# A decoder block on one core: the gates of its recurrence as pairs of 64-row matmuls, their evictions by halves

## The chip, the core and the metric

The kernel runs on one core of a Trainium2 chip. TensorE (PE) multiplies matrices into PSUM; VectorE (DVE), ScalarE (ACT) and GpSimd (POOL) do the elementwise work; SyncE (SP) issues most of the DMAs, ACT and POOL a few. The engines run side by side, each through its own instructions in a fixed order, and wait for one another by semaphores. The metric is the device time of one execution in microseconds (us).

## The reference, cut to what matters

The kernel computes one decoder block on x of 2048 positions by 1024 channels, in float32: one input projection to 9216 columns, a branch of dilated attention, a branch with a gated linear recurrence, a merge, an output projection and a layer norm. The change touches the recurrence:

```python
def rg_lru(x, w_r, b_r, w_i, b_i, lam):      # w_r, w_i: (16 blocks, 64, 64)
    xb = x.reshape(B, S, 16, 64)
    r = sigmoid(einsum('bsgi,gij->bsgj', xb, w_r).reshape(B, S, C) + b_r)
    i = sigmoid(einsum('bsgi,gij->bsgj', xb, w_i).reshape(B, S, C) + b_i)
    log_a = -8.0 * r * softplus(-lam)
    a = exp(log_a)
    mult = sqrt(maximum(-expm1(2.0 * log_a), 0.0))
    u = mult * (i * x)
    # h_t = a_t * h_(t-1) + u_t over the positions
```

Both gate matrices are block-diagonal: 16 blocks of 64 channels that don't mix.

## The kernel before, in words

**Stages.** The first stage (to about 1454 us) computes the input projection in products of seven matrices for four (Strassen's scheme), and the recurrence beside it. Then come the attention, the projections of both branches, and the output with the layer norm. Each float32 operand is split into a rounded part and a rest, so every product takes three matmuls: high by high, high by rest, rest by high.

**Layout.** Channels lie on the 128 partitions, positions on the free axis, in 4 chunks of 512. The 1024 channels of the recurrence are 8 tiles of 128 (`i`), each with two of the 64-channel blocks. For each tile and chunk the coroutine `lru(i, c, ub)` does the convolution, the two gates, and the scan: 32 chains in all.

**The order.** The first stage is written out step by step. A step (a "tick") records one product of 12 matmuls (`product`, L602 is its matmul), then the loads and weight preparations that fall due (`events`), then what waiting chains may record (`run_chains`), then the eviction of the product's PSUM bank (`evacuate`). A chain yields an `Ask`: how many ticks it waits (`lag`, 1 if not given), how many free slots of SBUF it needs, and how many microseconds of ACT, DVE or POOL it means to use. `run_chains` grants it only while the budget of that tick (`left`, refilled by 2.75 us a tick for each engine) is above zero. So a changed `Ask` moves not only its own chain: what it leaves or takes of the budget moves the steps of other chains, with their DMAs. The order on each engine is then fixed.

**The gates.** A chain loads its gate weights (L438, L439) into a slot `gr` as two matrices of 128x128, each with two blocks of 64x64 on its diagonal and zeros beside them, and splits them into `gw` (L456 on ACT, L219 on DVE, the helper `tt`). It splits its input `v` into `vh` and `vl`. The matmuls are put off by one tick and recorded in the middle of a product: three for r into one PSUM bank `g`, three for i into another (L472 to L474). There are two such banks, and a flag keeps a second chain out until the first has recorded its evictions. ACT evicts both banks by tanh (L485, L486; sigmoid is made from tanh), and in the same step of the chain makes the exponential, an affine step and a second tanh of r (L487 to L489), while DVE forms (1 + ti) * v (L490). Square root (L494), scan and the rest follow in later steps.

**Other names.** `q` are the PSUM banks of the products (four of them), `hA`, `hS`, `l` the split weights of a product, `wA`, `wS` their raw loads (L226 is the helper's line for both the plain and the half-summed ones), `wl_scr` a scratch copy of `l` for the second half. `vtp` are transposes in the same stage. `s` (L981) and `o` (L1034) are matmuls of the attention, `yb` (L1281 to L1283) the projection that follows it.

Of the kernel before, what the change touches and what calls it, by code (L numbers as in the profile page):

```python
# [8 lines left out]
F32 = mybir.dt.float32  # L9
F32R = mybir.dt.float32r  # L10
AF = mybir.ActivationFunctionType
ALU = mybir.AluOpType
# [3 lines left out]
P = 128  # L16
# [4 lines left out]
CH = 512  # L21
# [10 lines left out]
def hybrid_block_kernel(ctx: ExitStack, tc: tile.TileContext, a: dict, out: bass.AP):  # L32
    nc = tc.nc
    sp, act, dve, pool, pe = nc.sync, nc.scalar, nc.vector, nc.gpsimd, nc.tensor

    def flat(t):
        return t.bitcast(F32)
# [39 lines left out]
    lr = cst.tile([P, 8, 8], F32, name="lr")  # L77
    act.dma_start(lr, a["lru_vec"])
    brh = cst.tile([P, 2, 8], F32, name="brh")
    sp2 = cst.tile([P, 8], F32, name="sp2")  # L80


# [41 lines left out]
    ps = stA.enter_context(tc.tile_pool(name="ps", bufs=2, space=PSUM))  # L124
# [93 lines left out]
    def tt(eng, out, in0, in1, op):  # L218
        eng.tensor_tensor(out=out, in0=in0, in1=in1, op=op)  # L219
# [201 lines left out]
    GLG, GW = {}, {}  # L421
# [5 lines left out]
    def lru(i, c, ub):  # L427
        nm = f"{i}_{c}"
        f = FT_U + i
# [5 lines left out]
        if bring_gw:  # L435
            yield Ask(lag=0, need=1, keep=1)
            gr = take("gr" + nm, F32)
            sp.dma_start(gr[:, 0:P], a["wr"][i])  # L438
            sp.dma_start(gr[:, P:2 * P], a["wi"][i])  # L439
        if c == 1 and i in put_off:  # L440
            yield Ask(lag=4)
        yield Ask(lag=0, need=1, keep=6, cond=lambda: gate["live"] < 2 and begun[i] == c, ACT=1.3, DVE=2.7)
# [5 lines left out]
        for j in range(1, 4):  # L448
            dve.scalar_tensor_tensor(out=v, in0=ub[:, j:j + CH], scalar=lrn[:, j, i:i + 1], in1=v,
                                     op0=ALU.mult, op1=ALU.add)  # L450
        act.activation(ubs[:, i, c + 1, 0:3], ub[:, CH:CH + 3], AF.Copy)
        ub_free.append(ub)
        if bring_gw:
            yield Ask(ACT=.4, DVE=.4, lag=2, need=1, keep=1)
            w = GW[i] = take("gw" + nm)
            act.activation(w[:, 0:2 * P], gr[:, 0:2 * P], AF.Copy)  # L456
            tt(dve, w[:, 2 * P:], gr[:, 0:2 * P], flat(w[:, 0:2 * P]), ALU.subtract)
            give(gr)
        yield Ask(lag=0, cond=lambda: gated[i] == c)
        gw = GW[i].rearrange("p (l j f) -> p l j f", l=2, j=2)  # L460
        yield Ask(need=2, keep=1, ACT=.66, DVE=.75)
        vh, vl = take("vh" + nm), take("vl" + nm)
        act.activation(vh, v, AF.Copy)
# [3 lines left out]
        pg = []  # L467

        def gates():
            for j in range(2):  # L470
                g = ps.tile([P, CH], F32, tag="g", name=f"g{j}{nm}", bufs=2)
                pe.matmul(g, gw[:, 0, j], vh, start=True, stop=False)  # L472
                pe.matmul(g, gw[:, 0, j], vl, start=False, stop=False)
                pe.matmul(g, gw[:, 1, j], vh, start=False, stop=True)  # L474
                pg.append(g)
            give(vh, vl)
            if c in ((0, 3) if i in put_off else (1, 3)):
                give(GW[i])

        pe_later(1, gates)  # L480
        gated[i] = c + 1
        yield Ask(lag=2, need=3, keep=1, ACT=3.3, DVE=.75)
        gate["busy"] = False
        tr, ti, e = take("tr" + nm, F32), take("ti" + nm, F32), take("e" + nm, F32)
        act.activation(tr, pg[0], AF.Tanh, scale=0.5, bias=brh[:, 0, i:i + 1])  # L485
        act.activation(ti, pg[1], AF.Tanh, scale=0.5, bias=brh[:, 1, i:i + 1])  # L486
        act.activation(e, tr, AF.Exp, scale=sp2n[:, i:i + 1], bias=sp2n[:, i:i + 1])  # L487
        act.activation(e, e, AF.Identity, scale=0.5, bias=half_t)
        act.activation(tr, tr, AF.Tanh, scale=sp2[:, i:i + 1], bias=sp2[:, i:i + 1])  # L489
# [3 lines left out]
        s, w = take("sq" + nm, F32), take("nw" + nm, F32)  # L493
# [12 lines left out]
        h = take("h" + nm, F32)  # L506
# [11 lines left out]
        g = GLG.pop((i, c))  # L518
# [165 lines left out]
    for s, pl in enumerate(plan):  # L684
        if pl[0] and pl[4] == "ug":
            i = pl[1][1][0] - FT_U
# [70 lines left out]
    at(base[len(seq)] - 10, drop_cs)  # L757
    at(base[len(seq)] + 12, lambda: load_cs(1))

    HALF = (slice(0, 64), slice(64, P))  # L760
    USLOT = (("X3", "X2"), ("X0", "X4"), ("Y0", "X1"))
    VSLOT = {(0, 0): "X5", (2, 0): "Y1", (1, 0): "Y2", (0, 1): "X5", (2, 1): "Y1", (1, 1): "Y2"}

# [87 lines left out]
    def consts():  # L851
        dve.tensor_scalar(out=bh, in0=b72, scalar1=0.5, scalar2=None, op0=ALU.mult)
        dve.tensor_scalar(out=bn, in0=b72, scalar1=-1.0, scalar2=None, op0=ALU.mult)
        dve.tensor_scalar(out=bq, in0=b72[:, 0:64], scalar1=0.25, scalar2=None, op0=ALU.mult)
        dve.tensor_scalar(out=brh, in0=lr[:, 5:7, :], scalar1=0.5, scalar2=None, op0=ALU.mult)
        dve.tensor_scalar(out=lrn, in0=lr[:, 0:4, :], scalar1=-1.0, scalar2=None, op0=ALU.mult)
        dve.memset(ubs, 0.0)
        dve.memset(hst, 0.0)
# [62 lines left out]
    n = len(where)  # L921
# [35 lines left out]
    def scores(i):  # L957
# [40 lines left out]
    def turn(i, w):  # L998
# [303 lines left out]
    for n in range(32):  # L1302
        c, f = divmod(n, 8)
# [223 lines left out]
```

## Time and profile before

| | |
|---|---|
| median of 3 runs | 2132.93 us (2130.52 to 2132.96) |
| profiled execution | 2130.19 us, its span 2128.4 us |
| PE busy | 2093.8 us (98% of the span), 12016 matmuls |
| DVE, ACT, POOL busy | 1672.6 (79%), 1078.8 (51%), 457.6 us (22%) |
| gate matmuls (L472 to L474) | 192, started between 111.6 and 1404.3 us |
| tanh evictions of the gates (L485, L486) | 64, 688 and 684 ns each (median) |
| loads of the activation table | 66, 1283 ns each |

In the rows of the profile a line gives start, duration, engine, source line, operation, out<-in, shapes and a count of merged instructions; in brackets stands how long the engine had been idle and what ended it. "PEld" is the weight load of a matmul, "SPq" and "ACTq" an issue of a DMA by that engine. A matmul's record goes on after the next one has started, so the pace of a stream is read from the starts.

### The profile page before, as it was taken

The numbers are of one execution on the slowest core, as the hardware profiler recorded it, in microseconds if no ns is written. First come the engines' busy times: TensorE is split into PE (matmuls) and PEld (weight loads), VectorE is DVE, ScalarE is ACT, GpSimd is POOL, SyncE is SP. The second block draws the span as 40 slices with busy tenths as digits, with TensorE's granted clock in tenths as the row PEclk, the third lists the DMA queues.
The fourth block names the chain that finished last, engine by engine and source line by source line (L and its number), as shares of the span: only waits on it lengthen the run. The fifth ranks groups of instructions, "written<-read, shape, count | busy, mean of one in ns | idle before, by whom it ended". The sixth has DMA issues, their size and how long they took to land.

```text
span 2128.4 us, 35700 instructions
## 1 busy us (share of the span) xinstructions
PE 2093.8 (98%) x12016; PEld 1745.9 (82%) x12016; DVE 1672.6 (79%) x3193; ACT 1078.8 (51%) x2284; POOL 457.6 (22%) x397
## 2 busy tenths in 40 slices
PE   8999999999999999999999999999999999999998
PEld 7888888888878888888888888888888888878887
DVE  8888889799789867787787887886999645476667
ACT  6355445357356566546557656657999411121100
POOL 1001011011011002121221221223535444332120
PEclk9999999999999999999999999999999999999999
DMA  9987997988988876677778788879998688874431
GB/s 273 275 267 218 290 261 238 272 265 250 278 271 257 305 220 196 221 226 219 249 251 270 262 256 254 256 227 383 289 310 262 210 280 281 290 246 162 163 109 70
DMA packets 348263, 525.72 MB, mean 247 GB/s; under 512 B 123568, under 2 KB 156336, under 8 KB 344240
## 3 DMA queue, kind: packets, MB, share of 16 engines
q1 hardware_dynamic: 330368, 491.64, 71.3%
q0 software_dynamic: 10080, 18.35, 5.4%
q10 hardware_dynamic: 7632, 13.44, 1.7%
q8 instruction: 96, 1.57, 0.3%
q14 instruction: 87, 0.71, 0.1%
HBM read 318.18 MB, written 190.45 MB: 239 GB/s over the span
## 4 chain that ended last, share of the span: by engine, by line
PE 60%; ACT 6%; DMA 3%; DVE 2%; issue 1%; SPq 1%; POOL 0%; DVEq 0%; ACTq 0%
PE q L602 37%; ACT p L996 4%; PE z L1393 3%; PE z L1391 3%; PE z L1392 3%; PE yb L1281 2%; PE yb L1282 2%; PE yb L1283 2%; PE o L1034 1%; ACT ptb L1019 1%; PE ya L1361 1%; PE ya L1360 1%; PE ya L1359 1%; PE s L981 1%; DMA yb_scr<-gB 1%; DVE p L988 1%
## 5 line engine op out<-in xcount | busy, mean ns | idle before, releaser
L602 PE MATMUL q<-xT,hS 128*128 128x512 f32 x1680 | 518.8, 390 | 0.0
L602 PE MATMUL q<-xT,l 128*128 128x512 f32 x1120 | 436.0, 389 | 0.0
L602 PE MATMUL q<-xB,hA 128*128 128x512 f32 x1248 | 387.3, 392 | 5.7 <-ACT xB L207 5.7
L602 PEld LDWEIGHTS q<-xT,hS 128*128 128x128 f32 x1680 | 314.1, 188 | 64.3
L602 PE MATMUL q<-xB,l 128*128 128x512 f32 x904 | 352.9, 390 | 0.5 <-DMA l<-wl_scr 0.4
L602 PEld LDWEIGHTS q<-xB,hA 128*128 128x128 f32 x1248 | 234.1, 188 | 54.4 <-ACT xB L207 5.7
L602 PEld LDWEIGHTS q<-xT,l 128*128 128x128 f32 x1120 | 210.2, 188 | 44.3
L602 PEld LDWEIGHTS q<-xB,l 128*128 128x128 f32 x904 | 170.1, 188 | 37.5 <-DMA l<-wl_scr 0.8
L264 ACT ACTIVATE hA<-wA 128x512 fp32r<-128x512 f32 x218 | 135.5, 623 | 82.1 <-DMA wA<-in_w_in_dram 44.0
L602 PE MATMUL q<-xB,hS 128*128 128x512 f32 x560 | 173.5, 391 | 2.2 <-DVE v L219 2.2
L996 ACT ACTIVATE p<-p,sta 128x256 f32<-128x256 f32 (+1 forms) x384 | 172.2, 455 | 5.9 <-DVE sta L988 5.2
L602 PE MATMUL q<-xT,hA 128*128 128x512 f32 x560 | 172.8, 390 | 0.0
L237 POOL DMA_DIRECT2D wS<-in_w_in_dram x70 | 61.1, 935 | 477.6 <-DMA wS<-in_w_in_dram 120.0
L264 ACT ACTIVATE hS<-S 128x512 fp32r<-128x512 f32 x175 | 109.0, 623 | 87.9 <-DVE S L219 48.4
L219 POOL TENSOR_TENSOR S<-S,wA 128x512 f32<-128x512 f32 x35 | 45.6, 1303 | 445.8 <-DVE S L219 319.1
L602 PEld LDWEIGHTS q<-xB,hS 128*128 128x128 f32 x560 | 104.2, 188 | 23.8 <-issue 2.6
L602 PEld LDWEIGHTS q<-xT,hA 128*128 128x128 f32 x560 | 104.7, 188 | 21.9 <-issue 0.4
L988 DVE CUSTOM_DVE_ANT_0 p<-s,mask 128x256 f32<-128x256 f32 (+1 forms) x384 | 118.8, 360 | 4.6 <-PE s L981 3.6
L1393 PE MATMUL z<-wo,ml 128*128 128x512 f32 (+1 forms) x264 | 101.1, 383 | 0.8 <-DVE ml L1378 0.8
L1391 PE MATMUL z<-wo,mh 128*128 128x512 f32 (+1 forms) x264 | 101.1, 383 | 0.1
L1392 PE MATMUL z<-wo,mh 128*128 128x512 f32 (+1 forms) x264 | 101.0, 383 | 0.0
L1281 PE MATMUL yb<-h,wl 128*128 128x512 f32 x256 | 100.3, 392 | 0.0
(199 smaller groups left out, 4182.1 us busy)
## 6 DMA issues: line engine op xcount, KB each, us to landing
wA<-in_w_in_dram SPq DMA_DIRECT2D x253, 256.0 KB, 5.0
wl_scr<-l SPq DMA_DIRECT2D x105, 512.0 KB, 5.3
l<-wl_scr SPq DMA_DIRECT2D x105, 512.0 KB, 4.8
sw<-y SPq DMA_DIRECT2D x384, 64.0 KB, 3.1
wS<-in_w_in_dram SPq DMA_DIRECT2D x70, 256.0 KB, 4.8
wS<-in_w_in_dram POOLq DMA_DIRECT2D x70, 256.0 KB, 6.4
qh_scr<-hi SPq DMA_DIRECT2D x48, 256.0 KB, 5.8
v_scr<-vs SPq DMA_DIRECT2D x48, 256.0 KB, 4.4
```

The lines of the kernel that those rows point to most:

```text
L219: eng.tensor_tensor(out=out, in0=in0, in1=in1, op=op)
L237: pool.dma_start(t, w_part(s, x), accum_op=ALU.add)
L264: act.activation(h, r, AF.Copy)
L602: pe.matmul(bank, w[:, ks], x[:, kk, xx], start=(first and i == 0), stop=(last and i == 11))
L988: dve.tensor_tensor_reduce(out=st["p", i, j][:, h, lo:256], in0=st["s", i, j // 2][h][:, j % 2, lo:256], in1=mask[:, lo:256], scale=1.0, s ...
L996: act.activation(p, p, AF.Exp, scale=-1.0, bias=s[:, h:h + 1], accum_out=s[:, 2 + h:3 + h])
L1281: pe.matmul(yb, WL[f][:, 0, k], xx[:, 0], start=(k == 0), stop=False)
L1282: pe.matmul(yb, WL[f][:, 0, k], xx[:, 1], start=False, stop=False)
L1283: pe.matmul(yb, WL[f][:, 1, k], xx[:, 0], start=False, stop=(k == 7))
L1391: pe.matmul(z, mh[:, k], w[:, 0, hs], start=(k == 0), stop=False)
L1392: pe.matmul(z, mh[:, k], w[:, 1, hs], start=False, stop=False)
L1393: pe.matmul(z, ml[:, k], w[:, 0, hs], start=False, stop=(k == 7))
```

## The change

The gate matrices are no longer padded to 128x128. The upper 64 partitions hold, side by side, the blocks of r and of i for the tile's first 64 channels; the lower 64 hold those of its second 64 channels, i first and then r. A matmul takes 64 partitions of weights and of input and fills all 128 partitions of a bank: bank 0 gets r above and i below, for the first 64 channels; bank 1 gets i above and r below, for the second 64. Six matmuls of 64 rows, alternating between the upper and the lower half, take the place of six of 128 rows.

The evictions go by halves, so that r and i each end on their own channels' partitions: four tanhs of 64x512 instead of two of 128x512, two of which read PSUM on one half of the partitions and write SBUF on the other. The biases `brh` are arranged to match by four small DMAs on ACT's queue at the start. The step of the chain that held the tanhs and what follows is cut in two: the four tanhs ask for 2.5 us of ACT, and a tick later at the earliest the exponential, the affine step, the second tanh and DVE's product ask for 2.0 us of ACT and 0.75 of DVE. The gate weights are loaded by four DMAs of 64x64 instead of two of 128x128, and their split covers half the columns.

```diff
+    HALF = (slice(0, 64), slice(64, P))
+    for hs, os in (HALF, HALF[::-1]):
+        act.dma_start(brh[hs, 0], a["lru_vec"][hs, 5])
+        act.dma_start(brh[hs, 1], a["lru_vec"][os, 6])
...
-            sp.dma_start(gr[:, 0:P], a["wr"][i])
-            sp.dma_start(gr[:, P:2 * P], a["wi"][i])
+            for hs, n in ((HALF[0], ("wr", "wi")), (HALF[1], ("wi", "wr"))):
+                for j in range(2):
+                    sp.dma_start(gr[hs, HALF[j]], a[n[j]][i, hs, hs])
...
-            yield Ask(ACT=.4, DVE=.4, lag=2, need=1, keep=1)
+            yield Ask(ACT=.25, DVE=.25, lag=2, need=1, keep=1)
             w = GW[i] = take("gw" + nm)
-            act.activation(w[:, 0:2 * P], gr[:, 0:2 * P], AF.Copy)
-            tt(dve, w[:, 2 * P:], gr[:, 0:2 * P], flat(w[:, 0:2 * P]), ALU.subtract)
+            act.activation(w[:, 0:P], gr[:, 0:P], AF.Copy)
+            tt(dve, w[:, P:2 * P], gr[:, 0:P], flat(w[:, 0:P]), ALU.subtract)
...
-            for j in range(2):
-                g = ps.tile([P, CH], F32, tag="g", name=f"g{j}{nm}", bufs=2)
-                pe.matmul(g, gw[:, 0, j], vh, start=True, stop=False)
-                pe.matmul(g, gw[:, 0, j], vl, start=False, stop=False)
-                pe.matmul(g, gw[:, 1, j], vh, start=False, stop=True)
-                pg.append(g)
+            pg[:] = [ps.tile([P, CH], F32, tag="g", name=f"g{j}{nm}", bufs=2) for j in range(2)]
+            for k, (l, x) in enumerate(((0, vh), (0, vl), (1, vh))):
+                for hs, g in zip(HALF, pg):
+                    pe.matmul(g, gw[hs, l], x[hs], start=(k == 0), stop=(k == 2))
...
-        yield Ask(lag=2, need=3, keep=1, ACT=3.3, DVE=.75)
+        yield Ask(lag=2, need=2, keep=1, ACT=2.5)
         gate["busy"] = False
-        tr, ti, e = take("tr" + nm, F32), take("ti" + nm, F32), take("e" + nm, F32)
-        act.activation(tr, pg[0], AF.Tanh, scale=0.5, bias=brh[:, 0, i:i + 1])
-        act.activation(ti, pg[1], AF.Tanh, scale=0.5, bias=brh[:, 1, i:i + 1])
+        tr, ti = take("tr" + nm, F32), take("ti" + nm, F32)
+        for h, (hs, os) in enumerate((HALF, HALF[::-1])):
+            act.activation(tr[hs], pg[h][hs], AF.Tanh, scale=0.5, bias=brh[hs, 0, i:i + 1])
+            act.activation(ti[hs], pg[h][os], AF.Tanh, scale=0.5, bias=brh[os, 1, i:i + 1])
+        yield Ask(need=1, keep=1, ACT=2.0, DVE=.75)
+        e = take("e" + nm, F32)
         act.activation(e, tr, AF.Exp, scale=sp2n[:, i:i + 1], bias=sp2n[:, i:i + 1])
...
-        dve.tensor_scalar(out=brh, in0=lr[:, 5:7, :], scalar1=0.5, scalar2=None, op0=ALU.mult)
+        dve.tensor_scalar(out=brh, in0=brh, scalar1=0.5, scalar2=None, op0=ALU.mult)
```

Source lines after the change are higher by 4 to 6 (L602 becomes L608, L219 becomes L223).

PE, the first group of gates, before. The last two numbers in a name are a chain's chunk or a product's number and the tile's number; banks 1294 and 1298 are r and i.

```order
L473 MATMUL g_0_1294<-vl_0_1224,gw_0_1200 128x512
L474 MATMUL g_0_1294<-vh_0_1223,gw_0_1200 128x512
L472 MATMUL g_0_1298<-vh_0_1223,gw_0_1200 128x512
L473 MATMUL g_0_1298<-vl_0_1224,gw_0_1200 128x512
L474 MATMUL g_0_1298<-vh_0_1223,gw_0_1200 128x512
L602 MATMUL q_5_1287<-xT_423,hS_5_1192 128x512 x2
```

The same group on PE now:

```order
L478 MATMUL g_0_1301<-vh_0_1229,gw_0_1206 128x512
L478 MATMUL g_0_1300<-vl_0_1230,gw_0_1206 128x512
L478 MATMUL g_0_1301<-vl_0_1230,gw_0_1206 128x512
L478 MATMUL g_0_1300<-vh_0_1229,gw_0_1206 128x512
L478 MATMUL g_0_1301<-vh_0_1229,gw_0_1206 128x512
L608 MATMUL q_5_1293<-xT_427,hS_5_1198 128x512 x2
```

The first gate matmul stands ahead of each piece. The group has kept its place in the product; its matmuls now alternate between the banks.

ACT, the evictions of that group and what follows them, before (`hA`, `hS` are weight copies for coming products, which PE waits for in the end):

```order
L485 ACTIVATE tr_0_1342<-g_0_1294,brh 128x512
L486 ACTIVATE ti_0_1343<-g_0_1298,brh 128x512
L487 ACTIVATE e_0_1344<-tr_0_1342,sp2n 128x512
L488 ACTIVATE e_0_1344<-e_0_1344,half_t 128x512
L489 ACTIVATE tr_0_1342<-tr_0_1342,sp_201 128x512
L264 ACTIVATE hA_6_1372<-wA_6_1251 128x512
L494 ACT_TABLE_LOAD
```

The same place on ACT now:

```order
L489 ACTIVATE tr_0_1348<-g_0_1300,brh 64x512
L490 ACTIVATE ti_0_1349<-g_0_1300,brh 64x512
L489 ACTIVATE tr_0_1348<-g_0_1301,brh 64x512
L490 ACTIVATE ti_0_1349<-g_0_1301,brh 64x512
L268 ACTIVATE hA_6_1375<-wA_6_1257 128x512
L493 ACTIVATE e_0_1380<-tr_0_1348,sp2n 128x512
L494 ACTIVATE e_0_1380<-e_0_1380,half_t 128x512
L495 ACTIVATE tr_0_1348<-tr_0_1348,sp_205 128x512
```

Four tanhs stand where two stood, and the weight copy that came after the second tanh of r now comes before the exponential. The number of table loads is 66 as before.

SP at the last gate load of the first half, before (`k_scr` and `ql_scr` are stores of keys and queries, `gr7` the gate weights of tile 7, `wA22_32` and `wA12_32` weights of product 32):

```order
L339 DMA ql_scr6_100<-rp6_0_6303 128x512
L325 DMA k_scr6_101<-rp18_1_6329 128x512
L438 DMA gr7_0_6360<-in_wr_dram 128x128
L439 DMA gr7_0_6360<-in_wi_dram 128x128
L226 DMA wA22_32_6382<-in_w_in_dram 128x512
L226 DMA wA12_32_6384<-in_w_in_dram 128x512
```

The same place on SP now:

```order
L343 DMA ql_scr6_100<-rp6_0_6341 128x512
L444 DMA gr7_0_6397<-in_wr_dram 64x64
L444 DMA gr7_0_6397<-in_wi_dram 64x64 x2
L444 DMA gr7_0_6397<-in_wr_dram 64x64
L230 DMA wA22_32_6421<-in_w_in_dram 128x512
L230 DMA wA12_32_6423<-in_w_in_dram 128x512
L329 DMA k_scr6_101<-rp18_1_6394 128x512
```

The store of k has moved behind the two weight loads, since its chain was granted a tick later. Elsewhere in the first half of the stage other stores stand later than before in the same way, and no weight load has a store newly ahead of it; in the second half both occur.

More of the change, by code (lines that the diff above doesn't have):

```diff
@@ L453, in lru @@
         if bring_gw:
-            yield Ask(ACT=.4, DVE=.4, lag=2, need=1, keep=1)
+            yield Ask(ACT=.25, DVE=.25, lag=2, need=1, keep=1)
             w = GW[i] = take("gw" + nm)
-            act.activation(w[:, 0:2 * P], gr[:, 0:2 * P], AF.Copy)
-            tt(dve, w[:, 2 * P:], gr[:, 0:2 * P], flat(w[:, 0:2 * P]), ALU.subtract)
+            act.activation(w[:, 0:P], gr[:, 0:P], AF.Copy)
+            tt(dve, w[:, P:2 * P], gr[:, 0:P], flat(w[:, 0:P]), ALU.subtract)
             give(gr)
         yield Ask(lag=0, cond=lambda: gated[i] == c)
-        gw = GW[i].rearrange("p (l j f) -> p l j f", l=2, j=2)
+        gw = GW[i].rearrange("p (l f) -> p l f", f=P)
         yield Ask(need=2, keep=1, ACT=.66, DVE=.75)
@@ L758, in hybrid_block_kernel @@
     at(base[len(seq)] + 12, lambda: load_cs(1))
-    HALF = (slice(0, 64), slice(64, P))
     USLOT = (("X3", "X2"), ("X0", "X4"), ("Y0", "X1"))
```

## The prediction

> **What bounds the kernel now.** I read the windows by stage first (columns: window, its length, then busy time and instructions of PE, PE's weight loads, DVE, ACT and POOL), then PE's waits, then one group of gate matmuls in the timeline.
>
> ```profile
> 0.00:1454.00 1454.00, 1445.61 (x6453) 1194.41 (x6454) 1192.98 (x1787) 807.63 (x1331) 228.03 (x196) 1.00 0.83 254
> 500.00:540.00 40.00, 40.00 (x178) 33.12 (x177) 39.30 (x62) 25.50 (x38) 6.05 (x6) 1.00 0.83 256
> ```
> ```profile
> PE q L602 <- DVE v L219: 2.2, 1, 2.2
> PE q L602 <- DMA l<-wl_scr: 0.4, 1, 0.4
> ```
> ```profile
> 893.41 0.39 PE L472 MATMUL g<-vh,gw 128*128 128x512 f32 x1
> ...
> 894.54 0.39 PE L474 MATMUL g<-vh,gw 128*128 128x512 f32 x1
> 894.77 0.62 PE L602 MATMUL q<-xT,hS 128*128 128x512 f32 x2
> ```
> The whole change lies in the first stage, 0 to 1454 us. PE is busy there for 1445.6 of 1454 us, and all its waits between 20 and 1450 us come to 2.6 us. So PE sets the pace: what it is spared there comes off the end, as long as ACT (808 us of 1454) and DVE (1193) keep feeding it. DVE has little to spare in places (39.3 of 40 us from 500 to 540). A matmul's record lasts 0.39 us, but the next one starts 0.227 us later: the six gate matmuls take 894.77 - 893.41 = 1.36 us. That is the price of one group; 32 groups (8 channel blocks by 4 chunks) take 43.5 us.
>
> **PE: six full matmuls become three pairs of 64 rows.** The nearest operation in the trace is the scores of the attention, also pairs of 64 contraction rows into two banks.
>
> ```profile
> 1501.59 0.28 PE L1034 MATMUL o<-ptb,V 128*64 128x128 f32 x2
> 1501.80 0.39 PE L981 MATMUL s<-B,A 64*128 64x256 f32 x2
> ...
> 1501.80 0.50 PE L981 MATMUL s<-B,A 64*128 64x256 f32 x4
> ...
> 1501.80 0.62 PE L981 MATMUL s<-B,A 64*128 64x256 f32 x6
> ...
> 1501.80 0.74 PE L981 MATMUL s<-B,A 64*128 64x256 f32 x8
> ```
> These are four answers over ever longer pieces of the same place: two matmuls have started and ended 0.39 us after 1501.80, four after 0.50, six after 0.62, eight after 0.74. So a pair of 256 columns goes by every 0.12 us. A 512-column matmul starts every 0.227 us, so 256 columns alone need 0.114: the second member of a pair costs next to nothing. For pairs of 512 columns I take 0.23 us, three of them 0.69 us. Bounds: 0.227 each, or 0.454 if the two did not overlap at all.
>
> The same rows show that changing between shapes costs something. The fourth matmul of 64 rows ends at 0.50; with the 0.28 us that such a record lasts, the second pair started about 0.22 us after the first, not 0.12: about 0.10 us for the first weight load, which nothing hides. The other pieces:
>
> ```profile
> 1454.66 0.39 PE L602 MATMUL q<-xB,l 128*128 128x512 f32 x1
> 1454.97 0.32 PE L981 MATMUL s<-B,A 64*128 64x128 f32 x1
> ...
> 1669.14 0.28 PE L1034 MATMUL o<-ptb,V 128*64 128x128 f32 x2
> ...
> 1669.35 0.50 PE L1281 MATMUL yb<-h,wl 128*128 128x512 f32 x1
> 1669.69 0.39 PE L1282 MATMUL yb<-h,wl 128*128 128x512 f32 x1
> ```
> Going in: 1454.97 comes 0.31 us after the last full matmul, 0.085 more than 0.227; with the 0.10 that is 0.19 us. Coming back: the first full matmul after a tiled one starts 0.20 to 0.21 us after it, where 128 columns at the pace above need about 0.11 with their load, so about 0.09 more; and its successor comes 0.34 us later instead of 0.227, 0.11 more: 0.20 us. Together 0.39 us a group. Bounds: nothing; or, each way, the whole rest of the record (0.39 - 0.227) and an unhidden load (0.188, next fence), 0.35 us.
>
> So 1.36 - 0.69 - 0.39 = 0.28, which I round down to 0.27 us a group: 32 x 0.27 = **8.7 us less**. Ends: 32 x 0.67 = 21 us less with free switches, 1 us more with 0.35 us each way.
>
> **ACT: four evictions of 64x512 for two of 128x512, and the chain in two steps.**
>
> ```profile
> L485 ACT ACTIVATE tr<-g,brh 128x512 f32<-128x512 f32 x32 | 21.9, 685 | 10.1 <-PE g L474 9.6 <-PE g L473 0.3
> L1019 ACT ACTIVATE ptb<-pt 128x512 f32<-128x512 f32 x44 | 25.7, 583 | 0.4
> L1019 ACT ACTIVATE ptb<-pt 128x256 f32<-128x256 f32 x20 | 7.4, 372 | 0.0
> L456 ACT ACTIVATE gw<-gr 128x256 fp32r<-128x256 f32 x16 | 6.5, 407 | 19.1 <-DMA gr<-in_wi_dram 19.1
> L474 PEld LDWEIGHTS g<-vh,gw x64: 187/188/188, 111.8 to 1404.1; 128*128 128x128 f32 x64
> ```
> ```profile
> 493.67 0.39 PE L472 MATMUL g<-vh,gw 128*128 128x512 f32 x1
> ...
> 497.56 0.68 ACT L485 ACTIVATE tr<-g,brh 128x512 f32<-128x512 f32 x1
> 498.12 0.69 ACT L486 ACTIVATE ti<-g,brh 128x512 f32<-128x512 f32 x1
> ...
> 503.19 0.39 PE L472 MATMUL g<-vh,gw 128*128 128x512 f32 x1
> ```
> No activation on 64 partitions is in this trace. Columns set the time (583 ns for 512, 372 for 256), so I take a half at the full 0.685 us: 2 x 0.685 x 32 = 44 us more on ACT, 852 of some 1445 us, 59% instead of 56%; the other end is no more time than now. It costs the end nothing if it hides under the products. Two covers could fail. First the gate banks: in the closest-spaced pair of groups ACT ends with them at 498.81 and PE writes them again at 503.19, 4.4 us later; 1.4 us fits. Second the weights and bank copies queued behind on ACT: the order shown with the change now puts one weight copy ahead of the three activations that follow the tanhs, which helps it. The smaller weights spare ACT and DVE at most 16 x 0.41 us each, off the path. The extra step delays the recurrence by one step of the order; nothing but its own successors waits for it. I cost all this at nothing.
>
> **The start: four small DMAs on ACT's queue ahead of its table load.**
>
> ```profile
> 0.80 0.41 ACTq L73 DMA_DIRECT2D b<-in_b_in_dram  x1
> 1.25 0.45 ACTq L78 DMA_DIRECT2D lr<-in_lru_vec_dram  x1
> 1.73 1.28 ACT L264 ACT_TABLE_LOAD   x1 [1.73 <-PEq L1516]
> 4.14 0.63 ACT L264 ACTIVATE hA<-wA 128x512 fp32r<-128x512 f32 x1 [1.12 <-DMA wA<-in_w_in_dram]
> 5.66 1.52 PE L602 MATMUL q<-xB,hA 128*128 128x512 f32 x2 [5.66 <-ACT xB L207]
> ```
> Four issues of 0.45 us push the table load from 1.73 to 3.53 and its end to 4.81. The first activation, now at 4.14 with 1.12 us of idle before it, comes 0.67 us later, and PE's first matmul follows it (bounds 0 and 1.8). I take **0.6 us more**.
>
> **SP: four loads of gate weights for two, and stores that move back.** The 32 more issues at some 0.4 us are 13 us of SP's queue. In the first half they matter less than what the order shows: the store of k that stood ahead of two weight loads now stands behind them.
>
> ```profile
> 571.54 4.34 SPq L336 DMA_DIRECT2D ql_scr<-rp  x1
> 575.98 3.60 SPq L325 DMA_DIRECT2D k_scr<-rp  x1
> 579.67 0.38 SPq L438 DMA_DIRECT2D gr<-in_wr_dram  x1
> 580.10 0.44 SPq L439 DMA_DIRECT2D gr<-in_wi_dram  x1
> 580.59 0.90 SPq L226 DMA_DIRECT2D wA<-in_w_in_dram  x2
> ```
> ```profile
> 585.38 0.69 DVE L219 TENSOR_TENSOR S<-S,wA 128x512 f32<-128x512 f32 x1 [5.18 <-issue]
> ...
> 584.57 0.39 PE L602 MATMUL q<-xT,l 128*128 128x512 f32 x1
> 587.15 0.70 PE L602 MATMUL q<-xB,hS 128*128 128x512 f32 x2 [2.20 <-DVE v L219]
> ```
> ```profile
> wA<-in_w_in_dram SPq DMA_DIRECT2D x253, 256.0 KB, 5.0
> ```
> This is PE's one real wait. The profile doesn't name what DVE waited 5.18 us for; a weight load issued at 580.59 that takes its median 5.0 us lands at 585.6, just there. Without the 3.60 us store ahead, and with two more small loads (0.8 us), it is issued 2.8 us earlier, and the wait (587.15 - 584.57 - 0.23 = 2.35 us) can vanish. Bounds: 2.35 less, or 0.8 more if the load isn't what is late. I take **2.0 us less**.
>
> **DVE where it is full.** From 500 to 540 us PE can't run ahead of DVE. Two groups stand just there (493.67 and 503.19), so 2 x 0.27 = 0.54 us at most is lost again, nothing at least; I take **0.4 us more**, since DVE is at 98% (39.3 of 40).
>
> Sum: -8.7 + 0.6 - 2.0 + 0.4 = **-9.7 us**, against the profiled execution's 2130.19 us (span 2128.4 and 1.8 around it): 2120.5. The median of the runs shown is 2.7 us above that execution, their lowest 0.3; half of it added gives **2122**.
>
> **Rivals.** *The switches eat the gain.* If each way costs the rest of the record and a whole load (0.35 us), a group takes 0.69 + 0.70 = 1.39 us: no gain, and 2130.2 + 1 + 0.6 - 2.0 + 0.4 = 2130. Against it stand 0.19 and 0.20 us in the rows above; for it, that the way back was seen only once, and after another shape. [...] Chance 0.13.
>
> *ACT becomes what PE waits for* (slower). In the rows of the gate banks above, the first tanh runs 3.9 us after the matmuls began (497.56 after 493.67), behind other work of ACT; 1.37 us more lands on whatever is queued next, a weight copy or an emptied bank. If PE feels it in every other group, 16 x 1.37 = 22 us: 2142. It outweighs the gain from 8 groups of 32 (9.7 / 1.37), and is measurably slower from 11. Against it: PE's waits in the stage are 2.6 us now, none on ACT. Chance 0.11.
>
> *The pairs don't overlap as hoped* (slower). If a pair's weights could not be loaded while the pair before still runs on the same rows, each pair would add 0.188 us: 32 x 3 x 0.188 = 18 us, 2120.5 + 18 = 2139. [...] The score rows speak against it (a pair every 0.12 us, on the same rows each time, shorter than a load). If the two halves ran one after the other, 32 x 0.39 = 12.5 us of switches would come on top of today's time, 2130.2 + 12.5 + 0.6 - 2.0 + 0.4 = 2142. Together 0.06.
>
> *The switches are free* between these shapes: 12 us better still, 2108. The rows speak against it; 0.05.
>
> **How the numbers follow.** The forecast has 0.65, with its own range from 2114 (switches half as dear: 32 x 0.2 = 6 us) to 2129 (the wait at 584 stays, and the medians' full 2.7 us). A measurement of this kernel tells about 0.2%, 4.3 us, from no change. Faster: 0.60 of the forecast and the free switches, 0.65. Same: 0.05 of the forecast, and the eaten gain, 0.18. Slower: ACT and the missing overlap, 0.17. The range runs from 2113 to 2139: outside lie the free switches (0.05), ACT (0.11) and the serial halves (0.03).
>
> **What would show it.** The six gate matmuls in three starts about 0.23 us apart, the first about 0.10 later; 1.09 us from the first gate matmul to where the stream is back on pace, counted against 1.36; eight to nine us less from 111 to 1404 us; ACT some 44 us busier in the stage, and none of PE's waits on it; PE's wait near 584 us gone; the first matmul at about 6.3 us. It is wrong if halves take less than 0.6 us on ACT, if PE begins to wait for a gate bank or for ACT's copies, or if the way back from 64 rows costs more than 0.3 us.

## The result, and the profile after

| | before | after |
|---|---|---|
| median of 13 runs each, side by side | 2129.65 us | 2133.32 us (2129.6 to 2138.68) |
| ratio after to before | | 1.0017, 95% interval 1.0009 to 1.0025 |
| profiled execution, its span | 2130.19, 2128.4 us | 2131.70, 2130.0 us |

The change made the kernel slower by 0.17%, some 3.7 us. That is less than the 0.2% that I called measurable, but the interval of the ratio leaves 1 out. The forecast was 2122 us, faster, so about 11 us stand between it and the result. As a change I had forecast 9.7 us less, and it came out 3.7 us more, 13.4 us apart: with 13 runs the kernel before has a lower median, 2129.65 us, than with the three runs that I reckoned from.

TensorE (PE) got what it was to get. First the windows of the first stage, then one group of gates in the timeline, both of the kernel after:

```profile
0.00:1454.00 1454.00, 1438.99 (x6438) 1170.36 (x6439) 1187.93 (x1784) 851.19 (x1394) 224.81 (x194) 1.00 0.82 252
```
```profile
499.70 0.39 PE L608 MATMUL q<-xT,l 128*128 128x512 f32 x1
500.02 0.50 PE L478 MATMUL g<-vh,gw 64*128 64x512 f32 x2
500.35 0.40 PE L478 MATMUL g<-vl,gw 64*128 64x512 f32 x2
500.59 0.39 PE L478 MATMUL g<-vh,gw 64*128 64x512 f32 x2
500.91 0.73 PE L608 MATMUL q<-xT,hS 128*128 128x512 f32 x2
501.48 0.39 PE L608 MATMUL q<-xT,l 128*128 128x512 f32 x1
```
The two halves of a pair start together (one row, x2). From the product's matmul at 499.70 to that at 501.48 it is 1.78 us; with six full matmuls it would be nine steps of 0.227, 2.04 us. That is 0.26 us a group, 8.4 us in 32 groups. The way in costs 0.09 and 0.10 us over the pace (0.32 for 0.227, 0.33 for 0.23), the way back 0.09 and 0.11.

ScalarE (ACT) pays what was reckoned: 851 us in the stage in place of 808. These are the groups by line and shape, after:

```profile
L490 ACT ACTIVATE ti<-g,brh 64x512 f32<-64x512 f32 x64 | 43.8, 685 | 2.0 <-PE q L608 0.7
L489 ACT ACTIVATE tr<-g,brh 64x512 f32<-64x512 f32 x64 | 43.7, 682 | 11.4 <-PE g L478 10.4
```
A half takes as long as a whole eviction, 0.68 us.

What was given back shows in PE's waits, and behind them in those of VectorE (DVE). PE's waits between 20 and 1450 us, after (engine and line waiting, who for: us in total, times, longest):

```profile
PE q L608 <- DVE v L223: 7.3, 4, 3.3
PE vtp L357 <- DVE y L554: 0.2, 1, 0.2
```
The waits for DVE were 2.2 us in one place. DVE's waits ahead of `S`, which reads the raw weights `wA`, in the first two lines before, in the others after. Under "issue" stands what the profile puts down to no releaser; before, these are the two waits at 425 and 585 us:

```profile
DVE S L219 <- DMA wA<-in_w_in_dram: 13.7, 8, 5.3
DVE S L219 <- issue: 10.7, 2, 5.5
```
```profile
DVE S L223 <- DMA wA<-in_w_in_dram: 31.5, 12, 7.6
DVE S L223 <- issue: 1.8, 1, 1.8
```
So they grew from 24.4 to 33.3 us in all. The two places that are dear for PE are at 430 us, where PE did not wait before, and at 590 us, the old wait of 584 us. (The longest single wait, 7.6 us at 267 us, PE does not feel.) The timeline of SyncE's queue (SP), of DVE and of PE at the second, after:

```profile
577.07 4.24 SPq L340 DMA_DIRECT2D ql_scr<-rp  x1
581.40 3.61 SPq L329 DMA_DIRECT2D k_scr<-rp  x1
585.06 0.54 SPq L444 DMA_DIRECT2D gr<-in_wr_dram  x1
585.65 1.75 SPq L444 DMA_DIRECT2D gr<-in_wi_dram  x2
587.44 0.59 SPq L444 DMA_DIRECT2D gr<-in_wr_dram  x1
588.13 1.00 SPq L230 DMA_DIRECT2D wA<-in_w_in_dram  x2
```
```profile
592.35 0.69 DVE L223 TENSOR_TENSOR S<-S,wA 128x512 f32<-128x512 f32 x1 [7.30 <-DMA wA<-in_w_in_dram]
```
```profile
590.33 0.39 PE L608 MATMUL q<-xT,l 128*128 128x512 f32 x1
593.98 0.81 PE L608 MATMUL q<-xB,hS 128*128 128x512 f32 x2 [3.26 <-DVE v L223]
```
The store of k still stands ahead of the gate loads and of `wA` here, as it did before, and the four loads take 3.07 us from the first issue to that of `wA` (585.06 to 588.13) where two took 0.92. `wA` is issued 7.5 us later than before, and PE stands still for 3.65 - 0.23 = 3.4 us in place of 2.35. At 430 us it is the same row of stores and loads, and PE waits 3.0 us.

After both waits the matmuls run at 0.427 us each for a while. The window behind the wait at 430 us:

```profile
434.00:437.40 3.40, 3.40 (x11) 1.82 (x11) 3.13 (x6) 2.38 (x4) 1.11 (x2) 0.50 0.69 243
```
The granted clock (the third number from the end) is 0.50 for 3.4 us: about eight matmuls lose 0.2 us each, some 1.6 us on top of the wait.

The other loss is at the start. ACT's queue, after:

```profile
1.74 0.53 ACTq L82 DMA_DIRECT2D brh<-in_lru_vec_dram  x1
2.30 0.61 ACTq L83 DMA_DIRECT2D brh<-in_lru_vec_dram  x1
2.94 0.62 ACTq L82 DMA_DIRECT2D brh<-in_lru_vec_dram  x1
4.09 0.49 ACTq L83 DMA_DIRECT2D brh<-in_lru_vec_dram  x1
4.62 1.28 ACT L268 ACT_TABLE_LOAD   x1 [4.62 <-DMA wA<-in_w_in_dram]
...
7.12 1.60 PE L608 MATMUL q<-xB,hA 128*128 128x512 f32 x2 [7.12 <-ACT xB L211]
```
The four issues take 0.49 to 0.62 us and one of them comes 0.5 us after the one before had ended; PE starts at 7.12 in place of 5.66. At the same time SP's first four loads of x (`xcB`) take longer to issue, before in the first line, after in the second:

```profile
1.25 1.84 SPq L213 DMA_DIRECT2D xcB<-in_xT_dram  x4
```
```profile
1.25 4.16 SPq L217 DMA_DIRECT2D xcB<-in_xT_dram  x4
```
So SP is through with them 2.3 us later.

How far PE is behind the kernel before, read from the start of the same product matmul in both traces (the n-th of 6072):

| n-th matmul, time before | after is later by | what lies in between |
|---|---|---|
| 1st, 6 us | 1.5 us | the start |
| 1680th, 409 us | 2.3 | six groups of gates (1.6 us gained), some 2.4 us lost in small pieces, 0.9 of them by 14 us |
| 1800th, 437 us | 6.6 | the wait at 430 us and the clock after it, one group of gates |
| 2400th, 576 us | 5.8 | two groups of gates |
| 2520th, 607 us | 8.1 | 590 us in place of 584 us, with the clock after it, one group of gates |
| 4800th, 1153 us | 4.9 | thirteen groups of gates |
| 6000th, 1438 us | 3.2 | nine groups of gates, some losses beside them |
| end of the span | 1.6 | before, the clock is 0.50 for 3.4 us from 1467 us, in the attention; after, it is not |

### The profile page after: what moved, and what is told of

It reads as the page before. It is cut to its first block, busy times and chain, and to the rows that moved or that the text cites. A ratio compares the mean times of both kernels' runs of the same rounds, so it can differ in the third digit from the quotient of the medians.

```text
span 2130.0 us, 35843 instructions
## 1 busy us (share of the span) xinstructions
PE 2088.4 (98%) x12016; PEld 1723.3 (81%) x12016; DVE 1671.7 (78%) x3193; ACT 1123.3 (53%) x2348; POOL 455.6 (21%) x397
## 4 chain that ended last, share of the span: by engine, by line
PE 77%; DMA 6%; ACT 6%; DVE 6%; SPq 2%; issue 2%; POOL 0%; DVEq 0%; ACTq 0%; POOLq 0%
PE q L608 57%; ACT p L1001 5%; PE z L1398 3%; PE z L1397 3%; PE z L1396 3%; PE o L1039 1%; PE yb L1286 1%; PE yb L1287 1%; PE yb L1288 1%; PE g L478 1%; DMA yb_scr<-gB 1%; ACT ptb L1024 1%; DMA wA<-in_w_in_dram 1%; PE ya L1365 1%; PE ya L1364 1%
## 5 line engine op out<-in xcount | busy, mean ns | idle before, releaser
L608 PE MATMUL q<-xT,hS 128*128 128x512 f32 x1680 | 520.9, 391 | 0.0
L608 PE MATMUL q<-xT,l 128*128 128x512 f32 x1120 | 436.0, 389 | 0.0
L608 PE MATMUL q<-xB,hA 128*128 128x512 f32 x1248 | 389.0, 393 | 7.4 <-ACT xB L211 7.1
L608 PEld LDWEIGHTS q<-xT,hS 128*128 128x128 f32 x1680 | 312.9, 188 | 69.0 <-issue 5.5
L608 PE MATMUL q<-xB,l 128*128 128x512 f32 x904 | 353.8, 391 | 0.1
L608 PEld LDWEIGHTS q<-xB,hA 128*128 128x128 f32 x1248 | 233.3, 188 | 59.7 <-ACT xB L211 7.6
L608 PEld LDWEIGHTS q<-xT,l 128*128 128x128 f32 x1120 | 210.2, 188 | 44.4
L608 PEld LDWEIGHTS q<-xB,l 128*128 128x128 f32 x904 | 170.3, 188 | 37.2 <-DVE l L223 1.0
L608 PE MATMUL q<-xB,hS 128*128 128x512 f32 x560 | 175.5, 395 | 7.3 <-DVE v L223 7.3
L608 PE MATMUL q<-xT,hA 128*128 128x512 f32 x560 | 173.1, 390 | 0.1
L223 POOL TENSOR_TENSOR S<-S,wA 128x512 f32<-128x512 f32 x35 | 45.6, 1303 | 430.3 <-DVE S L223 267.3
L608 PEld LDWEIGHTS q<-xB,hS 128*128 128x128 f32 x560 | 104.3, 189 | 31.6 <-issue 9.7
L608 PEld LDWEIGHTS q<-xT,hA 128*128 128x128 f32 x560 | 104.7, 188 | 23.5 <-issue 2.0
L223 DVE TENSOR_TENSOR l<-wA,hA 128x512 fp32r<-128x512 f32 x113 | 79.4, 703 | 30.8 <-ACT hA L268 30.6
```

Source lines behind the costliest of these rows:

```text
L608: pe.matmul(bank, w[:, ks], x[:, kk, xx], start=(first and i == 0), stop=(last and i == 11))
```

## The experiments

All are compared with the kernel before, run beside them on the same chip; its median was 2128.6 us in the first set of four, 2130.5 in the second, 2129.0 and 2130.5 in the last two pairs. So differences between kernels of different sets are given by the ratios too, as a share of 2129 us.

### Loads, start, and both

My theory after the result: PE's gain is real, and the loads on SP and the four small DMAs at the start take it away. The rivals: ACT's extra work or the steps of the chain cost it, or the pairs themselves.

`gr_one` is the changed kernel with one load per tile, from an input in which each tile's four blocks lie as they are wanted (the inputs' layout differs, nothing computed does):

```diff
-            for hs, n in ((HALF[0], ("wr", "wi")), (HALF[1], ("wi", "wr"))):
-                for j in range(2):
-                    sp.dma_start(gr[hs, HALF[j]], a[n[j]][i, hs, hs])
+            sp.dma_start(gr[:, 0:P], a["wg"][i])
```


> The changed kernel, but the gate weights of a tile come by one DMA of 128x128 (laid side by side beforehand) instead of four of 64x64. Queue theory: PE's gain of 8.4 us was given back because the four loads stand on SP's queue ahead of two weight loads of a product, for 2.6 and 3.1 us at 425 and 585 us, so that DVE and then PE waited 3.0 and 3.4 us there and the clock fell back for some 1.4 us each time. Then the wait near 430 goes, that near 590 falls to 2 us or less, and the time is 3 to 5 us under the kernel before (ratio 0.9977 to 0.9986). ACT theory: the 44 us more of ACT and the longer chain delay PE, and the loads don't matter: the time stays 2 to 5 us above the kernel before.

`brh_one` is the changed kernel without the four small DMAs: the arranged biases are two more columns of a load that is there anyway.

```diff
-    for hs, os in (HALF, HALF[::-1]):
-        act.dma_start(brh[hs, 0], a["lru_vec"][hs, 5])
-        act.dma_start(brh[hs, 1], a["lru_vec"][os, 6])
...
-        dve.tensor_scalar(out=brh, in0=brh, scalar1=0.5, scalar2=None, op0=ALU.mult)
+        dve.tensor_scalar(out=brh, in0=lr[:, 8:10, :], scalar1=0.5, scalar2=None, op0=ALU.mult)
```


> The changed kernel, but the biases of the gates are ordered beforehand in the one array that is loaded anyway, so that the four small DMAs at the start are gone. Queue theory: PE starts at 5.7 us instead of 7.1, the waits at 430 and 590 stay: 1.5 to 2.3 us less than the changed kernel, 1.5 to 2.5 us above the kernel before. If the start is hidden by something later, no change from the changed kernel.

`both_one` has both edits.

> Both of the former together: one load of gate weights a tile, no small DMAs at the start; pairs of 64 rows, four evictions and the two steps stay. Queue theory: the two gains add up, 5 to 7.5 us under the kernel before (ratio 0.9965 to 0.9977). ACT theory: at most the start's 1.5 to 2.3 us is regained, 1.5 to 2.5 us above the kernel before.

`before_four` is the kernel before with its two loads of 128x128 cut into four of 64x128, and nothing of the change.

```diff
-            sp.dma_start(gr[:, 0:P], a["wr"][i])
-            sp.dma_start(gr[:, P:2 * P], a["wi"][i])
+            for hs in (slice(0, 64), slice(64, P)):
+                sp.dma_start(gr[hs, 0:P], a["wr"][i, hs])
+                sp.dma_start(gr[hs, P:2 * P], a["wi"][i, hs])
```


> The kernel before, with each of its two gate weight loads cut into two halves of 64 rows (four DMAs of 64x128, rows of 512 bytes), nothing else changed. Queue theory: each set of loads holds SP 0.9 us longer or more; the wait near 584 grows from 2.4 to 3.3 us or more and the clock falls back there, a wait appears near 426: 2 to 6 us above the kernel before. If only the rows of 256 bytes made the loads slow, or if the loads aren't what DVE waits for: within 1 us of the kernel before.

| | median, us | ratio to before | 95% interval |
|---|---|---|---|
| gr_one | 2124.74 | 0.9984 | 0.9975 to 0.9992 |
| brh_one | 2124.32 | 0.9982 | 0.9973 to 0.9991 |
| both_one | 2119.59 | 0.9957 | 0.9944 to 0.9969 |
| before_four | 2136.35 | 1.0037 | 1.0024 to 1.0050 |

`gr_one` and `brh_one` are each faster than both kernels, and `both_one` most of all, by 9.0 us against before: about what I had forecast for the change, and more than the 5 to 7.5 us expected of it. The four ratios, with the changed kernel's 1.0017, give each edit twice. Four loads in place of one cost 7.0 us with the small DMAs at the start and 5.3 without them; the small DMAs cost 7.5 us with four loads per tile and 5.7 with one. Together they cost 12.8 us (13.7 by the medians), about the 13.4 us between the forecast change and the measured one.

The time of `gr_one` came as expected, but not its waits: PE still waits 1.2 us at 430 us and 2.5 at 588 us, where the first was to go and the second to fall to 2 us or less. Its clock does not fall after them: the mean granted clock of the trace is 0.999, and behind the second wait the matmuls start some 0.23 us apart.

The trace of `both_one` has no wait of PE between 20 us and the end of the stage. Its SP, DVE and PE at the place of the old wait:

```profile
572.67 3.71 SPq L326 DMA_DIRECT2D k_scr<-rp  x1
576.44 0.42 SPq L439 DMA_DIRECT2D gr<-in_wg_dram  x1
576.96 0.89 SPq L227 DMA_DIRECT2D wA<-in_w_in_dram  x2
```
```profile
581.44 0.69 DVE L220 TENSOR_TENSOR S<-S,wA 128x512 f32<-128x512 f32 x1 [2.73 <-DMA wA<-in_w_in_dram]
```
```profile
582.85 0.39 PE L603 MATMUL q<-xT,l 128*128 128x512 f32 x1
583.08 0.70 PE L603 MATMUL q<-xB,hS 128*128 128x512 f32 x2
```
`wA` is issued 11 us earlier than in the changed kernel, while PE's products are some 7.5 us earlier there (582.85 for 590.33): 3.7 us of lead. DVE waits 2.73 us in place of 7.30, and PE, at 583.08, not at all.

`before_four` shows the loads alone: 7.7 us, 0.37%, where 2 to 6 were expected. Its rows of 64x128 are as long as those of before, so it is the number of the loads. PE's waits and DVE's for `wA` are in sum nearly those of the changed kernel, but 4.6 us of PE's 6.2 stand in one place, at 587 us (another 7.8 us of DVE's stand under "issue"):

```profile
PE q L603 <- DVE v L219: 6.2, 4, 4.6
```
```profile
DVE S L219 <- DMA wA<-in_w_in_dram: 28.6, 13, 8.6
```
The surprise was `brh_one`: 9.0 us by the medians (7.5 by the ratios) against the changed kernel, where I expected 1.5 to 2.3. The wait at 430 us is gone in its trace; that near 590 us stays (3.4 us, at 583 us), without the half clock after it: the matmuls behind it start 0.23 us apart (587.22, 587.45). That trace is of the fastest of its eleven runs. The same issue of `ql_scr` that comes at 416.46 in the changed kernel comes there at 409.43: the changed kernel's SP is 2 us late at 10 us, 3.8 at 250, 6 at 388 and 7 at 416. So, in these two traces, a start that is 1.5 us late on PE goes with an SP that falls further and further behind.

### Start alone, one load alone

`before_start` is the kernel before with the four small DMAs of the biases, in the old arrangement:

```diff
+    for hs in (slice(0, 64), slice(64, P)):
+        act.dma_start(brh[hs, 0], a["lru_vec"][hs, 5])
+        act.dma_start(brh[hs, 1], a["lru_vec"][hs, 6])
...
-        dve.tensor_scalar(out=brh, in0=lr[:, 5:7, :], scalar1=0.5, scalar2=None, op0=ALU.mult)
+        dve.tensor_scalar(out=brh, in0=brh, scalar1=0.5, scalar2=None, op0=ALU.mult)
```


> Before with the four small DMAs of the biases on ACT's queue at the start, and nothing else of the change. Theory one (the late start also costs SP the lead that it needs at 420 and 584 us, where PE already waits once): first matmul at 7.1 us, SP some 2 us late from 10 us on and later still at 420 us, PE's waits for DVE longer: 3 to 7 us more than before, 2132 to 2136. Rival (only the first matmul is late): 1.4 us more, 2130.

`before_one` is the kernel before with one load of both matrices per tile.

```diff
-            sp.dma_start(gr[:, 0:P], a["wr"][i])
-            sp.dma_start(gr[:, P:2 * P], a["wi"][i])
+            sp.dma_start(gr[:, 0:2 * P], a["wg"][i])
```


> Before with one load of 128x256 per tile for the two of 128x128 (both gate matrices side by side in memory), and nothing else of the change. Theory one (each issue on SP ahead of the product's weights counts): the load of wA near 584 us is issued 0.4 us earlier at that place and up to 3 us earlier by the issues spared before it (7 x 0.44): PE's wait of 2.35 us there shrinks or goes, 1 to 2.5 us less, 2126 to 2127.6. Rival (the two stores of 4.3 and 3.6 us alone make that wait): within 0.5 us of before.

`before_start` took 2131.75 us, ratio 1.0008 (0.9999 to 1.0018): 1.3 us, the rival's number, and my theory's 3 to 7 us was wrong. `before_one` took 2128.32 us, ratio 0.9992 (0.9983 to 1.0001): about 2 us less, which fits the theory but does not exclude nothing. Between one load and four lie 0.9992 and 1.0037, 9.6 us. The start is cheap on the kernel before and dear in the changed one, whether that has four loads per tile (7.5 us) or one (5.7). So it is not the number of the loads that makes it dear. It moves SP in both kernels (the first four loads of x take 4.10 to 4.16 us to issue in place of 1.84); why the kernel before hardly feels that is open. In its trace with the small DMAs, PE's wait near 584 us is even shorter, 0.9 us in place of 2.35.

### The pairs alone

`both_six_full` is `both_one`, `after_six_full` the changed kernel, each with six full matmuls for the three pairs:

```diff
-                for hs, g in zip(HALF, pg):
-                    pe.matmul(g, gw[hs, l], x[hs], start=(k == 0), stop=(k == 2))
+                for g in pg:
+                    pe.matmul(g, gw[:, l], x, start=(k == 0), stop=(k == 2))
```


> The version both_one with the pairs alone undone: six matmuls of 128 rows in place of three pairs of 64, on the same packed weights (so r and i are mixed from both gates: the gates are wrong, everything else is as it was). Theory one (the pairs' gain reaches the end as soon as SP's queue costs nothing): 32 x 0.264 = 8.4 us more than both_one, about 2128. Rival (the gain is partly taken back by DVE and the DMAs, which pace the stage in places): less than 4 us more, below 2124.

> The changed kernel with the pairs alone undone (six matmuls of 128 rows on the same weights; the gates are wrong, all else as in the change). Theory one (the pairs' 8.4 us reach the end in the change too, and loads and start take them away beside it): 8.4 us more than the changed kernel, 2139 to 2143. Rival (the waits at 430 and 590 us swallow part of what PE is spared, since PE only arrives there sooner): 2 to 6 us more, 2135 to 2139.

`both_six_full` took 2128.75 us, ratio 0.9991 (0.9982 to 1.0000): 9.2 us more than `both_one` by the medians, 7.2 by the ratios. `after_six_full` took 2142.22 us, ratio 1.0051 (1.0039 to 1.0064): 8.9 us more than the changed kernel by the medians, 7.2 by the ratios. The 8.4 us that the trace shows on PE reach the end, as far as the noise of some 2 us lets one tell, within the change too. So everything else in the change costs 11.8 us (2142.22 against 2130.47; 10.9 by the ratio); loads and start, each alone on the kernel before (`before_four` 7.7, `before_start` 1.3), make 9.0 of that.

### ACT's halves and the split step

`both_whole` is `both_one` with two whole evictions:

```diff
-        for h, (hs, os) in enumerate((HALF, HALF[::-1])):
-            act.activation(tr[hs], pg[h][hs], AF.Tanh, scale=0.5, bias=brh[hs, 0, i:i + 1])
-            act.activation(ti[hs], pg[h][os], AF.Tanh, scale=0.5, bias=brh[os, 1, i:i + 1])
+        act.activation(tr, pg[0], AF.Tanh, scale=0.5, bias=brh[:, 0, i:i + 1])
+        act.activation(ti, pg[1], AF.Tanh, scale=0.5, bias=brh[:, 1, i:i + 1])
```


> The version both_one with two tanhs of 128x512 in place of four of 64x512 (r and i then stand on the wrong channels for half of the partitions: the output is not the reference's). Theory one (ACT's 44 us lie beside the products): the same as both_one within 1.5 us, 2118 to 2121, ACT busy 44 us less. Rival (halves cost the end something through ACT's queue): 3 us less or more than that, 2116.5 or below.

It took 2119.31 us (0.9946, 0.9933 to 0.9959), as `both_one` by the medians, 2.3 us less by the ratios, whose intervals overlap. ACT is 45 us less busy in the stage (814.8 for 859.9). So with the step cut in two the halves cost nothing that is clear of the noise. Within the changed kernel itself this was not measured.

`both_one_step` is `both_one` with the step of the chain in one piece:

```diff
-        yield Ask(lag=2, need=2, keep=1, ACT=2.5)
+        yield Ask(lag=2, need=3, keep=1, ACT=3.3, DVE=.75)
...
-        yield Ask(need=1, keep=1, ACT=2.0, DVE=.75)
```


> The version both_one with the step of the chain in one piece again (one request of 3.3 us of ACT, 0.75 of DVE and three slots, as before). The stores of k at tiles 5 and 7 then stand ahead of the weight loads again, each 3 to 4 us of SP's queue. Theory one (such a store costs only where PE waits, and both_one has no such place at tiles 5 and 7): within 1.5 us of both_one, 2118 to 2121. Rival (the stores that moved back were worth what I gave them at tile 7): 2 to 4 us more, 2121.6 or above.

It took 2130.16 us (1.0006, 0.9997 to 1.0015): 10.6 us more than `both_one` by the medians, 10.4 by the ratios, far beyond what either reading had. The stores of k that moved are one possible cause, though at tiles 5 and 7 their issues take 0.32 us each in its trace, not 3 to 4; ACT's 1.37 us more in a single step is another. `both_step_whole` adds the edit of `both_whole` to it and so takes the second away; the order on SP is the same in both kernels.

> The version both_one_step (pairs, one packed load, good start, the step of the chain in one piece) with two tanhs of 128x512 in place of the four halves (half of r and i then stands on the wrong channels). It tells why both_one_step lost 10 us against both_one. Theory A (the order: with the step in one piece the stores of k and others stand ahead of weight loads again, SP is 2 to 5 us later from 455 us on): the loss stays, 2128 to 2131. Theory B (1.37 us more of ACT in a single step holds ACT's weight copies up): the loss goes, 2119 to 2122.

It took 2121.73 us (0.996, 0.9946 to 0.9974), 8.4 us less than `both_one_step` (9.8 by the ratios). The loss is gone with the halves, so it is not the order of the stores: it takes the halves and the step in one piece together. How they cost it I read from DVE's waits; no run takes that link away by itself. The place is the product (1 + ti) * v, in `both_one_step`, in `both_step_whole`, and after:

```profile
DVE ti L490 <- ACT ti L485: 41.1, 20, 6.8
```
```profile
DVE ti L489 <- ACT ti L484: 17.8, 6, 5.3
```
```profile
DVE ti L496 <- ACT ti L490: 1.0, 1, 1.0
```
In one step DVE's product follows right behind the four halves and stands in DVE's queue until the last of them is through: 41 us of waits on an engine that has little to spare. In `both_one_step` the loads of `wA` near 575 us are issued at 580.26, in `both_step_whole` at 574.38, with the same issues ahead. DVE's results are what SP stores, and SP's `wA` is what DVE waits for next, so in this kernel what delays one can delay the other: between 540 and 585 us SP's two longest waits in `both_one_step` are for DVE, 5.1 and 3.3 us. With the step cut in two the product comes a tick later, and DVE waits 1 us.

### The loads on another queue

`after_act_loads` is the changed kernel with its four loads per tile issued by ACT.

```diff
-                    sp.dma_start(gr[hs, HALF[j]], a[n[j]][i, hs, hs])
+                    act.dma_start(gr[hs, HALF[j]], a[n[j]][i, hs, hs])
```


> The changed kernel with its four loads of gate weights per tile issued by ACT in place of SP; number, size and place in the program as they were. Theory one (it is SP's issues ahead of wA that cost, 4 x 0.59 us per tile): wA is issued some 2.4 us earlier at the places at 430 and 590 us, PE's waits there (2.8 and 3.3 us, with some 1.5 us each for the clock after them) shrink or go: 5 to 9 us less than the changed kernel, 2124 to 2128. Rival (the small DMAs cost by what they do in the DMA engines, whoever issues them): within 1.5 us of the changed kernel. A third way (ACT, held up 2.4 us per tile, is late with the weight copies): slower than the changed kernel.

It took 2132.07 us, ratio 1.0014 (1.0005 to 1.0024): no gain. That is the rival's number, but not clearly its reason. The wait at 430 us is gone, as the theory had it. At 590 us it has grown, to 4.3 us for 3.3, and PE has new waits near 160 us, behind this stretch of ACT:

```profile
150.75 0.49 ACTq L444 DMA_DIRECT2D gr<-in_wr_dram  x1
151.27 0.62 ACT L268 ACTIVATE hS<-wS 128x512 fp32r<-128x512 f32 x1
151.29 2.64 ACTq L444 DMA_DIRECT2D gr<-in_wi_dram  x2
153.96 0.61 ACTq L444 DMA_DIRECT2D gr<-in_wr_dram  x1
154.63 0.20 ACT L451 ACTIVATE ub<-ubs 128x3 f32<-128x3 f32 x1 [2.74 <-issue]
```
ACT is held up 2.74 us by its own issues, and PE's waits near 160 us are for DVE, 0.9 and 1.2 us. So probably something like the third way of the expectation took part of the first's gain; whether the small transfers also cost by themselves, this run does not tell.

## Why the prediction was wrong

**The pairs** (8.7 us less forecast): right, in price and in mechanism. 8.4 us on PE, 7.2 to 9.2 at the end. The switches cost 0.19 and 0.20 us as read from the attention's rows, so the rivals of free switches, of switches that eat the gain, and of pairs that don't overlap are all out. The same two halves of rows come again from pair to pair, and the third pair still starts 0.24 us after the second (500.59 for 500.35), without the 0.188 us of a weight load that this last rival would add.

**ACT at nothing**: right as far as `both_whole` shows, but I named the wrong cover. I looked for ACT's copies and the gate banks; by DVE's waits the one that would have waited is DVE's product behind the halves, and what covers it is the split step. Without the split the halves cost 8.4 us (9.8 by the ratios). I had the extra step down as a delay that costs nothing; it is what the halves need.

**The step that failed: SP.** "In the first half they matter less than what the order shows" is wrong twice. The piece of SP's order that I showed is that of tile 7; the wait at 584 us belongs to the loads ahead of product 29, tile 6, and there the store of k stands ahead of `wA` before and after. So nothing was taken away, and two loads were added. And where the store did move back, at tile 7, its issue had been short, 0.32 us and not the 3.60 that I priced. The row of before:

```profile
632.61 0.32 SPq L325 DMA_DIRECT2D k_scr<-rp  x1
```
I took 2.0 us less, with 0.8 more as the other end. Measured: 2.3 us more at that place, and 4.3 us more at 430 us, where the same stores stand ahead of tile 4's loads. There DVE already waited 5.5 us before, without PE feeling it, and I had not looked:

```profile
425.52 0.69 DVE L219 TENSOR_TENSOR S<-S,wA 128x512 f32<-128x512 f32 x1 [5.54 <-issue]
```
I priced a load at 0.4 us from the issues of before; the four of after have a median of 0.594 us. And I had not thought of the clock behind a wait. Alone, on the kernel before, two loads more cost 7.7 us. None of the rivals was this one: the slower ones had PE waiting for ACT or for its own weights. That 2133 lies between 2113 and 2139 is luck, for that end of the range came from those rivals. (The forecast's own upper end was summed wrongly too: 2120.5 with the wait at 584 us left in, 2.0, and the medians' 2.7 us is 2125, not 2129.)

**The start** (0.6 us more forecast): the right mechanism, too small. It is 1.46 us on PE, since the issues took 0.49 to 0.62 us and one came late, and I left out SP, whose first issues slowed beside them. At the end it is 1.3 us alone on the kernel before, but 5.7 to 7.5 by the ratios in the changed one, and why these differ is open.

**DVE where it is full** (0.4 us more): not measured by itself. That SP and DVE can hand their delays on to each other is, as I read the traces, the larger thing, and I had treated both terms as separate.

`both_one` shows the sum without loads and start: 8.7 + 2.0 - 0.4 = 10.3 us less was forecast for the rest, 9.0 came. The wait of 584 us is gone in it, but not for my reason: it stays in `before_one` (1.4 us) and in `both_six_full` (1.6 us), and is absent in `both_step_whole`, where the stores stand as before. `both_six_full` differs from `both_one` by the pairs alone; in its trace `wA` is issued 2.9 us later there (579.88 for 576.96), with PE 2.2 us later. These are single traces, so what removes the wait is open.

## What to carry to other kernels

When an engine is 99% busy and is fed through a chain of two others, look for what already waits without being felt (here DVE, 5.5 us at 425 us): there a further delay can land on the busy engine. Follow each added DMA to the tile and product whose load it is ahead of, by the numbers in the names, rather than by the look of a neighbouring place. Loads that the new layout of a matmul cuts into pieces can be laid out once in the input; here that, for the weights and the biases, turned 0.17% slower into 0.43% faster.

## What was not expected of the hardware

- An activation of 64x512 takes 682 to 685 ns, one of 128x512 684 to 685: half the partitions cost the same. I had taken it so without a row that showed it.
- Four DMAs of 64 rows of 32 bytes each, issued by ACT at the start, slowed SP's issues beside them: four in 4.10 to 4.16 us in the traces that have them (the changed kernel, `gr_one`, `before_start`), 1.84 in those that have not (before, `brh_one`, `both_one`).
- The clock's fall after a wait is not a matter of the wait's length alone. In `both_one_step` 2.59 us passed from one matmul's start to the next (583.78 to 586.37), and the matmuls behind it started 0.43 us apart (587.36, 587.79); after 2.86 us in `gr_one` and 3.75 in `brh_one` they started 0.22 to 0.23 us apart (589.38, 589.60; 587.22, 587.45). In the changed kernel the granted clock was 0.50 for 3.4 us after each of its two waits (434.0 to 437.4, 594.4 to 597.8). What besides its length decides whether the clock falls after a wait, no run here shows.
